# Attention scores of a tile in one two-bank buffer, and the softmax sum applied to the output

## The chip, the cores and the metric

The kernel runs on one core of a Trainium2 chip. The metric is the device time of one execution in microseconds (us). A core has TensorE (PE in the profile, its weight loads PEld), VectorE (DVE), ScalarE (ACT), GpSimd (POOL) and SyncE (SP, which issues most DMAs). Each engine runs its instructions in the order in which they stand and waits on semaphores for the others. TensorE writes to PSUM, which has eight banks of 512 float32 columns on each of 128 partitions.

## The reference

A trunk of two layers over 1024 positions of width 1024. Layer 0 mixes with two recurrent head groups (RWKV-7 and gated DeltaNet); layer 1 mixes with chunked attention. Each layer ends with an MLP and a gated per-layer embedding. The attention has 16 heads of 64. Queries and keys are normalised, and each chunk of 64 positions looks at itself and the eight chunks before it:

```python
rel = jnp.arange(CHUNK)[:, None] + pad - jnp.arange(band)[None, :]
bias = rel_bias[:, jnp.clip(rel, -C_MAX_REL, C_MAX_REL) + C_MAX_REL]
s = jnp.einsum('bqhd,bkhd->bhqk', q_c, k_b).astype(jnp.float32) + bias
s = jnp.where(valid, s, -jnp.inf)
prob = jax.nn.softmax(s, -1).astype(v.dtype)
return jnp.einsum('bhqk,bkhd->bqhd', prob, v_b)
```

The bias depends on the distance alone, and beyond 256 positions it is one constant for each head. Because softmax does not change when a constant is added to a whole row, that constant can be subtracted from all biases of a head.

## The kernel before

Only the attention stage of layer 1 matters here (`layer1_in`, L1590). Positions are taken in eight tiles of 128, two chunks each. A query tile m sees at most the five key tiles m-4 to m, with a masked quarter at each end. Heads are taken in pairs `pr`, and positions in halves `hf`, which gives 16 steps. A step has four blocks: two heads (`h`), and for each two query tiles (`blk`).

For a step, `attn_in` (L1680) computes q, k and v of a head pair for four tiles: 24 float32r matmuls of 384 columns into one of two dense banks (`dps`, `wq`), which ACT and DVE then read (`qk` L1713, `vs` L1717 and L1718). `attn_norm` (L1732) transposes q and k (also through a dense bank) and splits them into a high and a low part (`F`, `Ql`). `attn_block` (L1759) is the softmax block:

- For a query tile the scores of the last three key tiles, the near ones, go to a bank `sn` (two buffers); those of up to two far key tiles go to a bank `sf` (one buffer). Each score is two matmuls, against q's high and low part; `score` cuts a run of key tiles where the tile of normalised keys ends, every four key tiles.
- On the near scores DVE adds the bias table `toep` and takes the row maximum in one custom instruction, into the SBUF tile `pb` (L1809). The far scores have a constant bias, which POOL has subtracted from the table (L1767), so DVE only masks a corner (L1816) and takes their maximum (L1817). L1818 joins the two maxima and negates them (L1821 where there are no far scores).
- ACT takes the exponential of the far scores out of PSUM (L1819) and of the near ones in place (L1822), each with its row sum. DVE adds the sums (L1824) and takes the reciprocal of one column (L1825). ACT scales all of `pb` by it (L1826).
- TensorE transposes the probabilities into a bank `pt` (two buffers; L1846, recorded at L165). ACT rounds them to float32r and DVE subtracts (`ptile`, L317 and L318), and the output matmuls `po` accumulate values times probabilities (L1858, recorded at L161). After a head's second block ACT and DVE fold the two halves of `po` into `y` (L1867, L1868), and `y` is written out.

Two lanes take blocks in turn, so that one lane's softmax runs beside the other's and beside the dense matmuls of later steps. The program is written in the order that a small planner sets (`run`, L123): it counts the time of matmuls and, at each `yield`, lets a lane rest for the time in the table `LAT` (L34). `attn_block0` is the rest after each tile's softmax, `attn_block1` the rest before the transposes. A scheduler of the language then fixes each engine's order. Matmuls of all lanes are issued by the helpers at L161 and L165, so groups are told apart by their tiles. Behind the attention, from about 2385 us on, stand the dense stages of layer 1.

The eight PSUM banks of this stage are two dense ones, two `sn`, one `sf`, two `pt` and one `po` (tag `o`).

## Time and profile before

| | us |
|---|---|
| runs of the kernel: median (lowest to highest of 3) | 3195.7 (3192.25 to 3198.93) |
| profiled execution: span from the first to the last instruction | 3188.9 |
| what lies between that span and the runs' median | 6.8 |
| attention stage of layer 1 (1800 to 2385) | 585.0 |
| dense stages behind it (2385 to 3189) | 804.0 |

No time of its own is recorded for the profiled execution beside its span, so the median of the runs stands for it. In the profile's groups each row names the line, the engine, the operation, output tile <- input tiles, the shapes and the count, then the busy time and the mean of one instruction (ns), and then how long the engine sat idle just before them and on whom it waited. A row of the waits names who waited, for whom, the sum in us, how often and the longest.

### The profile page before, as it was taken

The numbers are of one execution on the slowest core, as the hardware profiler recorded it, in microseconds if no ns is written. First come the engines' busy times: TensorE is split into PE (matmuls) and PEld (weight loads), VectorE is DVE, ScalarE is ACT, GpSimd is POOL, SyncE is SP. The second block draws the span as 40 slices with busy tenths as digits, with TensorE's granted clock in tenths as the row PEclk, the third lists the DMA queues.
The fourth block names the chain that finished last, engine by engine and source line by source line (L and its number), as shares of the span: only waits on it lengthen the run. The fifth ranks groups of instructions, "written<-read, shape, count | busy, mean of one in ns | idle before, by whom it ended". The sixth has DMA issues, their size and how long they took to land.

```text
span 3188.9 us, 45834 instructions
## 1 busy us (share of the span) xinstructions
PE 3080.8 (97%) x17448; PEld 2580.6 (81%) x17448; DVE 2005.1 (63%) x4020; ACT 1405.7 (44%) x2640; POOL 531.1 (17%) x982
## 2 busy tenths in 40 slices
PE   7999999999999999999999899989999999999999
PEld 5887778877877888888888888888878888888887
DVE  6565675557748766655546576776768666655552
ACT  4343443334426555312123477777756554312121
POOL 6334443434500000000004210110200000000002
PEclk8999889999899999999999999999999999999999
DMA  3312112222336433523213210110256333522313
GB/s 121 94 60 63 47 40 71 64 62 78 119 107 200 148 122 109 189 94 105 93 53 126 70 36 32 48 39 16 76 177 215 139 119 109 190 100 93 106 47 106
DMA packets 144715, 309.58 MB, mean 97 GB/s; under 512 B 40944, under 2 KB 43120, under 8 KB 144496
## 3 DMA queue, kind: packets, MB, share of 16 engines
q1 hardware_dynamic: 126064, 273.10, 25.8%
q10 hardware_dynamic: 18432, 33.56, 2.7%
q8 instruction: 137, 2.24, 0.3%
q14 instruction: 82, 0.67, 0.1%
HBM read 232.16 MB, written 74.45 MB: 96 GB/s over the span
## 4 chain that ended last, share of the span: by engine, by line
PE 86%; DVE 8%; ACT 4%; DMA 1%; issue 1%; POOL 0%; SPq 0%; DVEq 0%; ACTq 0%
PE dps L161 71%; PE ch L161 2%; PE iz L161 2%; PE tp L161 1%; PE po L161 1%; PE pm L161 1%; PE py L161 1%; PE pt L165 1%; DVE ptile L318 1%; PE sn L161 1%; PE pp L161 1%; DVE pb L1809 1%; ACT pb L1822 1%; DMA wraw<-in_w_qkv 1%; PE sc L161 1%
## 5 line engine op out<-in xcount | busy, mean ns | idle before, releaser
L161 PE MATMUL dps<-r,act 128*128 128x512 f32 x3528 | 824.3, 392 | 0.0
L161 PEld LDWEIGHTS dps<-r,act 128*128 128x128 f32 x3528 | 662.1, 188 | 145.7
L161 PE MATMUL dps<-xg,whi 128*128 128x512 f32 x1280 | 435.1, 416 | 12.7 <-ACT xg L320 7.2
L161 PE MATMUL dps<-late,act 128*128 128x512 f32 x1536 | 352.9, 391 | 0.0
L161 PEld LDWEIGHTS dps<-late,act 128*128 128x128 f32 x1536 | 288.5, 188 | 63.1
L161 PE MATMUL dps<-wq,act 128*128 128x384 f32 x1536 | 304.5, 344 | 6.9 <-DVE vs L1718 3.5
L1466 POOL TENSOR_TENSOR pn<-pn,prs 128x512 f32<-128x512 f32 x32 | 45.2, 1415 | 1587.7 <-ACT prs L354 1492.5
L161 PEld LDWEIGHTS dps<-xg,whi 128*128 128x128 f32 x1280 | 245.1, 196 | 67.6 <-ACT xg L320 7.2
L161 PEld LDWEIGHTS dps<-wq,act 128*128 128x128 f32 x1536 | 265.5, 191 | 11.1 <-DVE vs L1718 5.5
L161 PE MATMUL dps<-xg,wlo 128*128 128x512 f32 x640 | 264.5, 414 | 1.5 <-DVE wlo L277 1.5
L1342 DVE TENSOR_TENSOR late<-late,dps 128x512 f32<-128x512 f32 x224 | 152.9, 685 | 150.9 <-PE dps L161 120.2
L1441 DVE TENSOR_TENSOR xw<-xw,dps 128x512 f32<-128x512 f32 x192 | 131.6, 686 | 148.5 <-PE dps L161 147.5
L1240 ACT CAST act<-act 128x1024 fp32r<-128x1024 f32 (+1 forms) x99 | 94.7, 963 | 284.9 <-DMA act<-in_w 158.2
L1240 ACT CAST act<-late 128x512 fp32r<-128x512 f32 x210 | 124.6, 618 | 140.5 <-PE dps L161 121.3
L1241 DVE TENSOR_TENSOR act<-late,act 128x512 fp32r<-128x512 f32 x210 | 139.9, 688 | 27.2 <-ACT act L1240 26.9
L161 PEld LDWEIGHTS dps<-xg,wlo 128*128 128x128 f32 x640 | 125.6, 196 | 28.0 <-DVE wlo L277 2.8
L161 PE MATMUL dps<-xw,act 128*128 128x512 f32 x576 | 138.9, 392 | 0.0
L276 ACT CAST whi<-wraw 128x1024 fp32r<-128x1024 f32 x78 | 81.6, 1046 | 120.6 <-PE dps L161 81.6
L161 PEld LDWEIGHTS dps<-xw,act 128*128 128x128 f32 x576 | 108.1, 188 | 24.1
L1241 DVE TENSOR_TENSOR act<-act 128x1024 fp32r<-128x1024 f32 (+1 forms) x99 | 109.9, 1115 | 20.8 <-ACT act L1240 20.1
L277 DVE TENSOR_TENSOR wlo<-wraw,whi 128x1024 fp32r<-128x1024 f32 x78 | 99.3, 1274 | 36.5 <-ACT whi L276 35.7
L161 PE MATMUL po<-ptile,vs 128*128 128x256 f32 (+1 forms) x576 | 103.7, 292 | 15.5 <-ACT ptile L317 7.1
(474 smaller groups left out, 5410.7 us busy)
## 6 DMA issues: line engine op xcount, KB each, us to landing
act<-in_w SPq DMA_DIRECT2D x68, 512.0 KB
hd<-late ACTq DMA_DIRECT2D x128, 256.0 KB
late<-in_w SPq DMA_DIRECT2D x60, 512.0 KB
wraw<-in_w_in SPq DMA_DIRECT2D x56, 512.0 KB
act<-hd SPq DMA_DIRECT2D x56, 512.0 KB
wraw<-in_w_out SPq DMA_DIRECT2D x21, 512.0 KB
wraw<-in_w_qkv SPq DMA_DIRECT2D x21, 512.0 KB
pn<-pnd SPq DMA_DIRECT2D x32, 256.0 KB
```

Source lines behind the costliest of these rows:

```text
L161: return self.nc.tensor.matmul(out, lhsT, rhs, start=start, stop=stop)
L165: return self.nc.tensor.transpose(out, in_, ident)
L276: nc.scalar.copy(hi, raw)
L277: nc.vector.tensor_tensor(lo, raw, hi.bitcast(F32), op=ALU.subtract)
L318: nc.vector.tensor_tensor(dst[:, 1, sl], src, dst[:, 0, sl].bitcast(F32), op=ALU.subtract)
L1240: A.copy(hi, s)
L1241: V.tensor_tensor(lo, s, hi.bitcast(F32), op=ALU.subtract)
L1342: V.tensor_tensor(r, t, u, op=ALU.add)
L1441: V.tensor_tensor(x[n][:, sl], x[n][:, sl], ps, op=ALU.add)
L1466: G.tensor_tensor(pn, pn, prs[:, sl], op=ALU.mult)
L1809: V.tensor_tensor_reduce(S, pn[:, 0:nn * P], toep[:, (3 - nn) * P:], op0=ALU.add, op1=ALU.max, scale=1.0, scalar=NEG, accum_out=mx[:, 0:1])
L1822: A.activation(S, S, AF.Exp, bias=mx[:, 2:3], accum_out=l[:, 0:1])
```

## The change

A query tile's scores, up to five key tiles or 640 columns, now go into one buffer `sc` of two adjoining PSUM banks. There is one such buffer. `score` cuts a run also where it would cross from the first bank to the second. The bias table covers all five key tiles (640 columns instead of 384), with both masked corners written into it, so that nothing is subtracted from it. One custom DVE instruction adds the bias and takes the maximum of the whole row, one DVE instruction negates it, and one ACT instruction takes the exponential of the whole row with its sum.

The probabilities are not scaled. Instead DVE writes the reciprocal of the sum, repeated over 64 columns, into a tile `rl` (a query tile's rows by the head's 64 columns). After both heads of a step, TensorE transposes the four 128x128 pieces of `rl` into a dense bank, and DVE multiplies the step's output `y` by it. The bank that is left goes to `pt`, which has three buffers. Two entries of the planner's table change.

```diff
-    "attn_block0": 0.97,
-    "attn_block1": 4.45,
+    "attn_block0": 1.70,
+    "attn_block1": 3.00,
...
-            rbl = l1.tile([P, 16], F32, tag="rbl", name="rbl", bufs=1)
-            nc.sync.dma_start(out=rbl, in_=a["rb_last"].rearrange("(o c) -> o c", o=1).broadcast_to((P, 16)))
...
-                t = l1.tile([P, 3 * P], F32, tag="toep", name="toep", bufs=3)
+                t = l1.tile([P, 5 * P], F32, tag="toep", name="toep", bufs=3)
...
             t = st["toep"][h]
-            G.tensor_scalar(t, t, rbl[:, 2 * pr + h:2 * pr + h + 1], None, op0=ALU.subtract)
-            G.memset(t[0:64, 320:384], NEG)
+            G.memset(t[0:64, 576:640], NEG)
+            G.memset(t[64:128, 0:64], NEG)
...
-                e = min(n - o, 4 - j % 4)
+                e = min(n - o, 4 - j % 4, 4 - o % 4)
...
+        if h == 0 and blk == 0:
+            st["rl"] = sm.tile([P, 4, P], F32, tag="rl", name="rl", bufs=2)
         for m in (m0, m0 + 1):
-            n0 = max(0, m - 2)
-            nn = m - n0 + 1
             f0 = max(0, m - 4)
-            nf = n0 - f0
-            pn = psm.tile([P, HB], F32, tag="sn", name="sn", bufs=2)
-            score(pn[:, 0:nn * P], m, n0, nn)
-            mx = sm.tile([P, 4], F32, tag="mx", name="mx", bufs=4)
+            n = m - f0 + 1
+            ps = psm.tile([P, 2 * HB], F32, tag="sc", name="sc")
+            score(ps, m, f0, n)
+            mx = sm.tile([P, 2], F32, tag="mx", name="mx", bufs=4)
             pb = self.wp.tile([P, 5 * P], F32, tag="pb", name="pb", bufs=4)
-            S = pb[:, nf * P:(nf + nn) * P]
-            V.tensor_tensor_reduce(S, pn[:, 0:nn * P], toep[:, (3 - nn) * P:], op0=ALU.add, op1=ALU.max,
+            S = pb[:, 0:n * P]
+            V.tensor_tensor_reduce(S, ps[:, 0:n * P], toep[:, (5 - n) * P:], op0=ALU.add, op1=ALU.max,
                                    scale=1.0, scalar=NEG, accum_out=mx[:, 0:1])
-            l = sm.tile([P, 4], F32, tag="l", name="l", bufs=4)
-            if nf:
-                pf = psm.tile([P, HB], F32, tag="sf", name="sf")
-                score(pf[:, 0:nf * P], m, f0, nf)
-                if m >= 4:
-                    V.memset(pf[64:128, 0:64], NEG)
-                V.reduce_max(mx[:, 1:2], pf[:, 0:nf * P], axis=AX.X)
-                V.tensor_scalar(mx[:, 2:3], mx[:, 0:1], mx[:, 1:2], -1.0, op0=ALU.max, op1=ALU.mult)
-                A.activation(pb[:, 0:nf * P], pf[:, 0:nf * P], AF.Exp, bias=mx[:, 2:3], accum_out=l[:, 1:2])
-            else:
-                V.tensor_scalar(mx[:, 2:3], mx[:, 0:1], -1.0, None, op0=ALU.mult)
-            A.activation(S, S, AF.Exp, bias=mx[:, 2:3], accum_out=l[:, 0:1])
-            if nf:
-                V.tensor_tensor(l[:, 0:1], l[:, 0:1], l[:, 1:2], op=ALU.add)
-            V.reciprocal(l[:, 2:3], l[:, 0:1])
-            A.activation(pb[:, 0:(nf + nn) * P], pb[:, 0:(nf + nn) * P], AF.Copy, scale=l[:, 2:3])
+            V.tensor_scalar(mx[:, 1:2], mx[:, 0:1], -1.0, None, op0=ALU.mult)
+            l = sm.tile([P, 1], F32, tag="l", name="l", bufs=4)
+            A.activation(S, S, AF.Exp, bias=mx[:, 1:2], accum_out=l)
+            V.reciprocal(st["rl"][:, m % 4, hs], l.broadcast_to((P, 64)))
...
-            pt = psm.tile([P, HB], F32, tag="pt", name="pt", bufs=2)
+            pt = psm.tile([P, HB], F32, tag="pt", name="pt", bufs=3)
...
             V.tensor_tensor(y[hs], po[hs], tmp[hs], op=ALU.add)
             if h == 1:
+                pn = self.bank()
+                for m in range(4):
+                    self.tr(pn[:, m * P:(m + 1) * P], st["rl"][:, m, :], self.ident)
+                V.tensor_tensor(y, y, pn, op=ALU.mult)
...
-    rel = np.arange(P)[:, None] + 2 * P - np.arange(3 * P)[None, :]
+    rel = np.arange(P)[:, None] + 4 * P - np.arange(5 * P)[None, :]
     out["rb"] = f["attn_rel_bias"][0][:, np.clip(rel, -256, 256) + 256]
-    out["rb_last"] = f["attn_rel_bias"][0][:, 512]
```

**Scores on TensorE.** The order on PE at the first head's first block of step 7 (`F1` keys, `F0` and `Ql` the parts of q; the number behind a name is its buffer's; in brackets the engines that it waits for). Before:

```order
L161 MATMUL sn_18508<-F1_18037,F0_18489 128x256 [waits Activation_49]
L161 MATMUL sf_18517<-F1_18037,F0_18489 128x256
L161 MATMUL sn_18541<-F1_18037,F0_18489 128x128
L165 MATMUL pt_18561<-ident_62,pb_18427 128x128 [waits Activation_49]
L165 MATMUL pt_18572<-ident_62,pb_18427 128x128 [waits DVE_49]
L161 MATMUL sn_18508<-F1_18037,Ql_15464 128x256 [waits DVE_49]
L161 MATMUL sn_18508<-F1_18476,F0_18489 128x128
L161 MATMUL sn_18508<-F1_18476,Ql_15464 128x128
L161 MATMUL sf_18517<-F1_18037,Ql_15464 128x256
L161 MATMUL sn_18541<-F1_18037,Ql_15464 128x128
L161 MATMUL sn_18541<-F1_18476,F0_18489 128x256
L161 MATMUL sn_18541<-F1_18476,Ql_15464 128x256
```

With the change, the same block:

```order
L161 MATMUL sc_18335<-F1_17896,F0_18306 128x512 [waits Activation_49]
L161 MATMUL po_18241<-ptile_18318,vs_17396 128x256 [waits Activation_49]
L161 MATMUL sc_18335<-F1_17896,Ql_15462 128x512 [waits DVE_49]
L161 MATMUL sc_18335<-F1_18293,F0_18306 128x128
L161 MATMUL sc_18335<-F1_18293,Ql_15462 128x128
L161 MATMUL po_18241<-ptile_18318,vs_17396 128x256 [waits DVE_49]
L161 MATMUL po_18241<-ptile_18318,vs_17396 128x256 x2
L161 MATMUL po_18241<-ptile_18328,vs_17396 128x256 [waits Activation_49]
L161 MATMUL po_18241<-ptile_18328,vs_17396 128x256 [waits DVE_49]
L161 MATMUL po_18241<-ptile_18328,vs_17396 128x128 x2
L161 MATMUL sc_18371<-F1_17896,F0_18306 128x384 [waits DVE_49]
L161 MATMUL sc_18371<-F1_17896,Ql_15462 128x384
```

The two near tiles and the far one stood interleaved, each in a bank of its own; now the second tile's scores wait for DVE behind the first's, and the output matmuls of another block stand between.

**From the transposes to the output matmuls.** PE at the first head's second block of step 12 (`pt` transposes of the probabilities `pb`, `ptile` their split). Before:

```order
L165 MATMUL pt_20817<-ident_62,pb_20695 128x128 [waits Activation_49]
L165 MATMUL pt_20817<-ident_62,pb_20670 128x128
L165 MATMUL pt_20817<-ident_62,pb_20695 128x128
L165 MATMUL pt_20832<-ident_62,pb_20695 128x128 x2
L161 MATMUL dps_20915<-wq1_20762,act_15376 128x384
L161 MATMUL dps_20915<-wq0_20761,act_15376 128x384
L161 MATMUL po_20683<-ptile_20822,vs_19964 128x256 [waits Activation_49]
L161 MATMUL po_20683<-ptile_20822,vs_19964 128x256 [waits DVE_49]
```

With the change, the transposes of the same block:

```order
L165 MATMUL pt_20465<-ident_62,pb_20356 128x128 [waits Activation_49]
L165 MATMUL pt_20465<-ident_62,pb_20330 128x128
L165 MATMUL pt_20465<-ident_62,pb_20356 128x128
L165 MATMUL pt_20476<-ident_62,pb_20356 128x128 x2
L161 MATMUL dps_20520<-wq0_20425,act_15146 128x384
L161 MATMUL dps_20520<-wq1_20426,act_15146 128x384
L161 MATMUL sc_20455<-F1_20173,F0_20192 128x256 [waits DVE_49]
L161 MATMUL sc_20455<-F1_20173,Ql_15461 128x256
L161 MATMUL dps_20520<-wq0_20425,act_15146 128x384
L161 MATMUL dps_20520<-wq0_20425,act_15220 128x384
L161 MATMUL dps_20520<-wq1_20426,act_15220 128x384
L165 MATMUL pt_20528<-ident_62,pb_20392 128x128 [waits PE_49,Activation_49]
```

Two dense matmuls stood between the last transpose and the first output matmul of that block. Now scores, dense matmuls and another block's transpose come first; the block's output matmuls stand further down.

**The reciprocals' transposes.** PE at the end of step 4, with the change, and DVE at the same place:

```order
L161 MATMUL po_17469<-ptile_17585,vs_16634 128x256 [waits Activation_49]
L161 MATMUL po_17469<-ptile_17585,vs_16634 128x256 [waits DVE_49]
L161 MATMUL po_17469<-ptile_17585,vs_16634 128x128 x2
L165 MATMUL dps_17622<-ident_62,rl_17195 128x128 [waits DVE_49]
L165 MATMUL dps_17622<-ident_62,rl_17195 128x128 x3
L161 MATMUL sc_17569<-F1_17120,F0_17544 128x512 [waits Activation_49]
L161 MATMUL sc_17569<-F1_17120,Ql_15462 128x512 [waits DVE_49]
L161 MATMUL sc_17569<-F1_17531,F0_17544 128x128
L161 MATMUL sc_17569<-F1_17531,Ql_15462 128x128
L161 MATMUL dps_17646<-wq0_17377,act_14852 128x384 [waits DVE_49]
```

```order
L318 TENSOR_TENSOR ptile_17562<-pt_17557,ptile_17562 128x512 [waits Activation_49]
L318 TENSOR_TENSOR ptile_17585<-pt_17581,ptile_17585 128x384 [waits Activation_49]
L1752 SCALAR_TENSOR_TENSOR F1_17531<-dps_17526,vecs_60,F1_17531 64x512 [waits Activation_49]
L1752 SCALAR_TENSOR_TENSOR Ql_15462<-dps_17539,d_qg8_85,F0_17544 64x512 [waits PE_49,Activation_49]
L1854 TENSOR_TENSOR y_17455<-po_17469,otmp_17619 64x512 [waits Activation_49]
L1859 TENSOR_TENSOR y_17455<-y_17455,dps_17622 128x512 [waits DVE_49,PE_49]
L1807 ISA pb_17575,mx_17574<-sc_17569,toep_16629 128x640 [waits PE_49]
```

The transposes of `rl` and the multiply are new. The dense matmuls of `dps_17646` wait for DVE: their bank is the one that the multiply (L1859) reads.

More of the change, by code (lines that the diff above doesn't have):

```diff
@@ L1608, in layer1_in @@
             jobs = iter([(s, h, b) for s in range(16) for h in range(2) for b in range(2)])
-            self.run([self.attn_lane(steps, jobs, l1, rbl) for _ in range(2)] + [self.attn_norms(steps, l1), self.attn_ins(steps, l1)])
+            self.run([self.attn_lane(steps, jobs, l1) for _ in range(2)] + [self.attn_norms(steps, l1), self.attn_ins(steps, l1)])
     def attn_ins(self, steps, l1):
@@ L1657, in attn_norms, with attn_lane @@
             self.mark(("in", s), self.lat["norm"])
-    def attn_lane(self, steps, jobs, l1, rbl):
+    def attn_lane(self, steps, jobs, l1):
         for s, h, b in jobs:
             yield ("in", s)
-            yield from self.attn_block(s, *steps[s], h, b, l1, rbl)
+            yield from self.attn_block(s, *steps[s], h, b, l1)
     def weights3(self, odd):
@@ L1757, in attn_norm, with attn_block @@
             yield "attn_norm0"
-    def attn_block(self, s, pr, hf, h, blk, l1, rbl):
+    def attn_block(self, s, pr, hf, h, blk, l1):
         nc, psm, sm = self.nc, self.psm, self.sm
```

## The prediction

> **What bounds the kernel now.** I read the page first, then the busy time by stages, then the waits of TensorE inside the one stage that the change touches, then its groups of instructions and the chain that ended last.
>
> ```profile
> span 3188.9 us, 45834 instructions
> PE 3080.8 (97%) x17448; PEld 2580.6 (81%) x17448; DVE 2005.1 (63%) x4020; ACT 1405.7 (44%) x2640; POOL 531.1 (17%) x982
> core 0: us, PE busy (x) PEld busy (x) DVE busy (x) ACT busy (x) POOL busy (x), PEclk, DMA share, GB/s
> 1800.00:2385.00 585.00, 538.77 (x3329) 496.72 (x3327) 417.27 (x1320) 426.55 (x991) 70.58 (x69) 0.98 0.18 59
> 2385.00:3189.00 804.00, 798.84 (x3500) 653.89 (x3499) 479.61 (x658) 287.78 (x434) 21.69 (x16) 1.00 0.35 123
> ```
>
> The attention stage runs from about 1800 to 2385 us. Even there PE is the busiest engine, but it is busy for 538.8 of 585 us; behind it, in the dense stage, for 798.8 of 804. So the stage holds some 46 us of PE idle, and DVE (417 us) and ACT (427 us) are both near three quarters full, on short chains that feed PE. What matters is which of these chains PE waits for. These are the waits of the weight loads (PEld) and then of the matmuls (PE) in that window: us in total, times, longest.
>
> ```profile
> PEld po L161 <- ACT ptile L317: 12.2, 18, 2.0
> PEld po L161 <- DVE ptile L318: 10.6, 18, 1.6
> PEld pt L165 <- ACT pb L1826: 9.3, 11, 1.9
> PEld sf L161 <- ACT pb L1819: 6.8, 15, 1.2
> PEld pt L165 <- DVE ptile L318: 3.7, 8, 0.5
> PEld sn L161 <- DVE mx L1809: 3.1, 15, 0.3
> PE po L161 <- ACT ptile L317: 7.1, 12, 1.8
> PE pt L165 <- ACT pb L1826: 6.7, 9, 1.8
> PE po L161 <- DVE ptile L318: 6.6, 13, 1.4
> PE pt L165 <- DVE ptile L318: 4.3, 8, 1.5
> PE sf L161 <- ACT pb L1819: 3.3, 7, 1.0
> ```
>
> Three of the five chains are touched: the transposes `pt` wait for the scaled probabilities (L1826) or for a free `pt` bank; the far scores `sf` wait until the exponential has read their only bank (L1819); the output matmuls `po` wait for the split of the transposes. A PE row begins only after the modelled end of the last matmul, a PEld row as soon as no weight is loading, so I price a removed wait by PEld and keep the PE rows as the lower bound.
>
> **The change part by part: TensorE's own work.** The spacing of matmuls is read from the chain of waits, where they run without a gap: start, us, what.
>
> ```profile
> 2001.32 0.46 PE pt L165 x4
> 2001.78 3.47 PE dps L161 x20
> 2005.26 0.40 PE sf L161 x4
> 2008.38 0.93 PE po L161 x8
> 2374.51 4.56 PE dps L161 x20
> ```
>
> That is 0.115 us for a transpose, 0.10 to 0.116 for 128 and 256 columns, 0.174 for 384 and 0.228 for 512. The order has the scores before as 192 matmuls of 128 columns, 192 of 256 and 128 of 384 (63.8 us), and now as 224, 96, 96 and 64 of 512 (64.8 us): +1.0. The new transposes of the reciprocals are 4 in each of 16 steps, 64 x 0.115 = +7.4. Together **+8.4 us** of PE work, in a stage where nothing hides PE.
>
> **DVE and ACT.** First groups by line with all shapes together, then single shapes: xcount, busy us, mean ns, idle before.
>
> ```profile
> L1826 ACT ACTIVATE pb<-pb,l 128x640 f32<-128x640 f32 (+4 forms) x128 | 86.4, 693 | 16.6 <-DVE l L1825 13.9 <-DVE ss L1727 1.6 <-DVE mx L1821 0.4
> L1819 ACT ACTIVATE pb<-sf,mx 128x256 f32<-128x256 f32 (+1 forms) x80 | 36.2, 452 | 42.0 <-DVE mx L1818 41.6
> L1819 ACT ACTIVATION_READ_ACCUMULATOR pb<-sf,mx 128x1 f32 x80 | 15.8, 197 | 0.0
> L1817 DVE TENSOR_REDUCE mx<-sf 128x1 f32<-128x256 f32 (+1 forms) x80 | 31.2, 390 | 0.9
> L1824 DVE TENSOR_TENSOR l<-l 128x1 f32<-128x1 f32 x80 | 13.2, 165 | 27.8 <-ACT pb L1822 27.5
> L1816 DVE MEMSET sf<- 64x64 f32 x64 | 7.2, 112 | 28.9 <-PE sf L161 28.4
> L1818 DVE TENSOR_SCALAR mx<-mx 128x1 f32<-128x1 f32 x80 | 16.6, 207 | 1.1
> L1821 DVE TENSOR_SCALAR mx<-mx 128x1 f32<-128x1 f32 x48 | 6.5, 144 | 0.3
> L1825 DVE RECIPROCAL l<-l 128x1 f32<-128x1 f32 x128 | 20.2, 160 | 8.2 <-ACT pb L1822 6.1
> L1867 ACT COPY otmp<-po 64x512 f32<-64x512 f32 x32 | 18.6, 581 | 3.5 <-PE po L161 2.7
> ```
>
> ```profile
> L1809 DVE CUSTOM_DVE_ANT_0 pb<-sn,toep 128x384 f32<-128x384 f32 x96 | 51.6, 551 | 8.9 <-PE pt L165 6.4 <-PE sn L161 1.8
> L1809 DVE CUSTOM_DVE_ANT_0 pb<-sn,toep 128x128 f32<-128x128 f32 x16 | 4.5, 281 | 2.5 <-PE pt L165 1.9 <-PE sn L161 0.6
> L1822 ACT ACTIVATE pb<-pb,mx 128x384 f32<-128x384 f32 x96 | 58.6, 610 | 4.3 <-DVE mx L1821 4.3
> L1826 ACT ACTIVATE pb<-pb,l 128x640 f32<-128x640 f32 x64 | 53.3, 833 | 15.6 <-DVE l L1825 13.5 <-DVE ss L1727 1.6
> L318 DVE TENSOR_TENSOR ptile<-pt,ptile 128x512 fp32r<-128x512 f32 x80 | 53.5, 683 | 11.0 <-ACT ptile L317 9.9
> ```
>
> ACT loses the scaling (86.4), the far exponential (36.2) and its sum (15.8). The one that is left grows from 384 to 640 columns; the 640-column row of L1826 stands for it, 833 - 610 = 0.22 us more, 64 times, and about half as much 16 times: +16. Net -122 us, 427 to about 304.
>
> DVE loses 31.2 + 13.2 + 7.2, and 80 x (207 - 144) ns = 5.0. The bias-and-maximum costs (551 - 281)/256 = 1.05 ns a column, so 640 columns take 0.82 us: +0.27 x 64 and +0.135 x 16 = 19.4. The multiply of the output is 16 times a 512-column row of 0.68: 11.0. The reciprocal now writes 64 columns, which the trace does not show. Below it costs what it costs now, 0.16. Above I put the 512-column row, 0.68, as if each column took eight. I take plain streaming, 0.16 + 64 x 1.05 ns = 0.23, because the one-column reciprocal is no dearer than the one-column add (160 against 165 ns): +8.6. Net about -18 us, at worst 128 x 0.52 = 67 us instead of 8.6, which is +41.
>
> The Trainium skill (VectorE: DVE Perf Modes, "First, the fixed hardware budget") speaks against the change here: it says that a reciprocal is an iterative divide with a repeat count of 8. By that, 64 columns would be 512 passes, an estimate of some 0.53 us at its 0.96 GHz; no run here shows a wide one yet.
>
> None of DVE's or ACT's busy time sets the end; it works through PE's waits. POOL loses 13 bias shifts off any chain, and the wider bias table is 128 KB more for each of 16 loads where DMA is 18% busy; I cost both at nothing.
>
> **Waits that go.** (1) `pt` on the probabilities. From a score's last matmul to a transposable tile was 0.55 + 0.39 + 0.21 + 0.45 + 0.20 + 0.61 + 0.20 + 0.17 + 0.16 + 0.83 = 3.8 us of instructions; now it is 0.82 + 0.14 + 0.83 + 0.20 = 2.0. The planner's gap shrinks too, from 0.97 + 4.45 = 5.4 to 1.70 + 3.00 = 4.7, so slack grows from 1.6 to 2.7: three quarters of 9.3, **-7.0**. (2) `pt` on a free bank: there are three, and in the new order no transpose of probabilities waits for DVE: **-3.7**. (3) The `sf` bank is gone: **-6.8**. (4) `po` on the split. Between the last transpose of a tile and the first output matmul that waits for ACT, the old order has under 1 us of PE work in 37 of 119 places, the new one in 13 of 125; for the DVE half it is under 2 us in 37 of 96 and now in 20 of 139. ACT's queue is also more than a quarter shorter. I take 60% of 12.2 + 10.6: **-13.7**. Sum -31.2; by the PE rows the same shares give -20.8.
>
> **Waits that come.** (5) There is one two-bank score buffer, so the next tile's first score matmul waits until DVE has read the last one, with all of PE's queue behind it. Before, `sn` had two buffers. Old order: 17 of 113 waits had under 1 us of PE work as cover, and 3.1 us were lost, which fits a turn of 0.92 us. The read is 0.27 longer now, a turn of 1.19; the new order has 16 of 121 under 1 us and 24 under 1.5, and the shortfalls to 1.19 sum to 9.7: **+6.6**. (6) The reciprocals' transposes hold one of the two dense banks until the output is multiplied. Copy 0.58, add and multiply 0.68 each, with the handovers 2.5 us; the next user of that bank comes 1.3 to 2.7 us of PE work after the last output matmul in five of the 16 steps, later elsewhere: shortfalls of **+3.5**.
>
> Sum: 8.4 - 31.2 + 6.6 + 3.5 = **-12.7 us**. On the span that is 3176.2. The median of the runs is 3195.7, 6.8 above this span, so I predict **3183 us**. With the PE rows for the removed waits it would be -2.3, 3193.
>
> **The rivals.** *More comes back.* All of (1) to (4) go, 42.6 instead of 31.2: -24, 3172. For it speaks that ACT loses more than a quarter of its work; against it, that DVE, which a third of these waits name, loses little.
>
> *DVE takes it back: no change.* If the reciprocal is near its upper bound, DVE goes to 458 of some 575 us, and a reciprocal stands in DVE's order ahead of the score read or the split that PE needs. A turn 0.5 longer in half of the score reads (their shortfalls at 1.7 us sum to about 22) adds 6, and about 4 on the split: -3, 3193. The skill's rule on the reciprocal would end here.
>
> *The single score buffer decides: slower.* With two lanes sharing it, one DVE instruction of 0.68 us ahead of the read makes the turn 2 us; 36 of 121 reads have less cover, and the shortfalls sum to 31.8, so +28.7 instead of +6.6. With the removed waits at their PE price: 8.4 - 20.8 + 28.7 + 3.5 = +20, 3215. It decides from a turn of about 1.5 us on. For it: DVE is 71% busy. Against it: the old `sn` waits show a longest of 0.3 us.
>
> **How the numbers follow.** A measurement of this kernel tells about 0.2%, 6.4 us, from no change. Forecast (-6.4 to -20, 3176 to 3189): 0.38. More: 0.19. No change: 0.23. Slower: 0.20. So faster 0.57, same 0.23, slower 0.20. The range takes in the larger gain with the waits for `vs` gone too (some 9 us below 3172) and most of the slower case: 3160 to 3212.
>
> **What would show it.** Right: no wait of `pt` on the score bank's readers or on DVE, `po` waits for ACT and DVE under 10 us together in the PEld rows, `sc` on the score read near 10 us, ACT near 300 us in the stage, and a stage some 13 us shorter with the work behind it unchanged. Wrong: `sc` waits of 20 us or more, a wide reciprocal near 0.6 us with waits behind it, or dense matmuls waiting for the output's multiply in most steps.

## The result and the profile after

The changed kernel takes 3177.97 us (median of 4 runs, 3171.28 to 3180.88) against 3195.55 of the kernel before beside it (4 runs, 3192.25 to 3198.93). The ratio is 0.9937, with a 95% interval of 0.9923 to 0.9951: 0.63% or some 20 us faster (by the medians 17.6). The forecast was 3183, a gain of 12.7.

The page of the changed kernel, the execution's span and the engines' busy time:

```profile
span 3176.5 us, 45473 instructions
PE 3082.7 (97%) x17480; PEld 2587.2 (81%) x17480; DVE 2028.7 (64%) x3812; ACT 1307.4 (41%) x2352; POOL 515.4 (16%) x982
```

The span is 12.4 us shorter, less than the runs say. The stage began 6.4 us later in this execution (1777.1 us against 1770.7), although the change touches nothing before it. The odd one is the execution of the kernel before: in the other 13 traces of this document the stage begins between 1771.3 and 1785.3 us. The changed kernel's profiled execution took 3178.18 us, 1.7 more than its span. If the kernel before has about as much between the two, its profiled execution took some 3191 us, less than any of its runs, and most of the 6.8 us between its span and its median is that. So I compare stages. The attention stage is taken from the first read of a query bank (`qk`) to the first load for the residual add behind it (L1250), a place in the program and not a time. Its windows, of the kernel before and then of the changed one, with the columns of the windows in the prediction:

```profile
1770.70:2388.50 617.80, 570.79 (x3510) 527.80 (x3509) 430.31 (x1349) 434.82 (x1011) 73.70 (x72) 0.98 0.18 58
```

```profile
1777.10:2373.00 595.90, 563.62 (x3519) 526.06 (x3518) 453.88 (x1138) 335.09 (x721) 58.48 (x72) 0.98 0.19 62
```

The stage is 21.9 us shorter and what follows it 3.1 longer (800.4 to 803.5): -18.8. The 3.1 are work that changed sides: 3496 matmuls stand behind the border instead of 3484, with 798.3 us of PE busy instead of 795.3. DVE works 23.6 us more and ACT 99.7 less. The weight loads' waits in this stage, after the change (engine, tile and line, what was waited for: us, times, longest):

```profile
PEld sc L161 <- DVE mx L1807: 7.7, 18, 1.0
PEld pt L165 <- ACT pb L1811: 7.0, 11, 1.8
PEld po L161 <- ACT ptile L317: 6.7, 11, 1.2
PEld po L161 <- DVE ptile L318: 4.2, 7, 1.2
...
PEld dps L161 <- DVE y L1859: 3.2, 5, 1.0
```

The output matmuls' waits for the split have halved (22.8 to 10.9). Those for the far bank and for a free `pt` bank are gone. The waits for the score buffer (`sc`) and for the output's multiply (`y`, L1859, which holds a dense bank) are new. The groups of the new work, shapes kept apart:

```profile
L1812 DVE RECIPROCAL rl<-l 128x64 f32<-128x64 f32 x128 | 69.7, 546 | 25.1 <-ACT pb L1811 24.6
...
L1811 ACT ACTIVATE pb<-pb,mx 128x640 f32<-128x640 f32 x64 | 53.4, 835 | 45.2 <-DVE mx L1809 44.8
L1807 DVE CUSTOM_DVE_ANT_0 pb<-sc,toep 128x640 f32<-128x640 f32 x64 | 52.0, 813 | 18.0 <-PE sc L161 17.4
```

The 640-column instructions cost what was predicted (0.83 and 0.82 us). The reciprocal of 64 columns does not: 546 ns, where I took 0.23.

**How the runs below are compared.** All runs stand in one table. "Against before" is the ratio to the kernel before in the same series, less one, times 3196 us; a ratio's interval is about 4.5 us to each side, so a difference between two rows of different series is known to some 6 us. The last four columns are of one profiled execution: the stage as above; the sum of all PEld waits in it; the clock loss, which is the stage's length times one less the granted clock, summed over slices of 20 us; and what is left.

| kernel | median us | ratio (95%) | against before | stage | PEld waits | clock loss | rest |
|---|---|---|---|---|---|---|---|
| before | 3195.6 | | | 617.8 | 73.5 | 12.4 | 531.9 |
| after | 3178.0 | 0.9937 (0.9923-0.9951) | -20 | 595.9 | 51.0 | 10.4 | 534.5 |
| e4_merge_only | 3152.9 | 0.9866 (0.9854-0.9879) | -43 | 567.5 | 36.0 | 1.8 | 529.7 |
| e3_defer_only | 3208.8 | 1.0044 (1.0029-1.0059) | +14 | 631.7 | 70.9 | 24.0 | 536.8 |
| e13_no_scale | 3147.8 | 0.9842 (0.9829-0.9856) | -50 | 561.8 | 32.0 | 1.8 | 528.0 |
| e10_wide_recip | 3168.6 | 0.9908 (0.9895-0.9922) | -29 | 586.8 | 51.3 | 8.8 | 526.7 |
| e6_one_recip | 3167.0 | 0.9913 (0.9899-0.9928) | -28 | 584.9 | 44.4 | 6.8 | 533.7 |
| e11_both | 3191.2 | 0.9981 (0.9970-0.9992) | -6 | 608.1 | 61.3 | 10.6 | 536.2 |
| e1_old_rests | 3167.4 | 0.9899 (0.9884-0.9914) | -32 | 585.1 | 42.0 | 8.8 | 534.3 |
| e12_merge_old_rests | 3158.4 | 0.9888 (0.9873-0.9903) | -36 | 578.4 | 45.1 | 6.8 | 526.5 |
| e2_before_new_rests | 3207.5 | 1.0034 (1.0022-1.0045) | +11 | 626.0 | 73.7 | 23.6 | 528.7 |
| e5_pt2 | 3182.3 | 0.9962 (0.9949-0.9976) | -12 | 597.8 | 57.7 | 3.6 | 536.5 |
| e8_pt1 | 3235.9 | 1.0132 (1.0117-1.0147) | +42 | 641.1 | 90.1 | 22.6 | 528.4 |
| e9_pt1_sc2 | 3275.4 | 1.0253 (1.0235-1.0271) | +81 | 683.5 | 109.8 | 61.8 | 511.9 |

The rest is the check on this split. In the six kernels that transpose the reciprocals it is 533.7 to 536.8 (mean 535.3), and in those that do not, e9 aside, 526.5 to 531.9 (mean 528.6). The difference of 6.7 is near the 7.4 us that the prediction gave the 64 transposes. In e9, 14.6 us of the clock loss fall inside waits and so are counted twice; counted once, its rest is 526.5, like the others, whose rests rise by 0 to 4 us in the same way. So stage times are PE's work, plus its waits, plus a clock that falls after waits.

### The profile page after: what moved, and what is told of

It is laid out like the page before. It is cut to its first block, busy times and chain, and to the rows that moved or that the text cites. A ratio compares the mean times of both kernels' runs of the same rounds, so it can differ in the third digit from the quotient of the medians.

```text
span 3176.5 us, 45473 instructions
## 1 busy us (share of the span) xinstructions
PE 3082.7 (97%) x17480; PEld 2587.2 (81%) x17480; DVE 2028.7 (64%) x3812; ACT 1307.4 (41%) x2352; POOL 515.4 (16%) x982
## 4 chain that ended last, share of the span: by engine, by line
PE 86%; DVE 7%; ACT 3%; DMA 2%; issue 1%; POOL 1%; SPq 0%; ACTq 0%; DVEq 0%; POOLq 0%
PE dps L161 71%; PE ch L161 2%; PE iz L161 2%; PE sc L161 2%; PE po L161 1%; PE tp L161 1%; PE pm L161 1%; PE py L161 1%; PE pt L165 1%; PE pp L161 1%; DVE pb L1807 1%; DVE ptile L318 1%; ACT pb L1811 0%; PE st L161 0%; PE dps L165 0%
## 5 line engine op out<-in xcount | busy, mean ns | idle before, releaser
L161 PEld LDWEIGHTS dps<-wq,act 128*128 128x128 f32 x1536 | 266.1, 191 | 11.4 <-DVE vs L1716 4.5
L1811 ACT ACTIVATE pb<-pb,mx 128x640 f32<-128x640 f32 (+4 forms) x128 | 89.5, 699 | 84.2 <-DVE mx L1809 82.1
L1241 DVE TENSOR_TENSOR act<-act 128x1024 fp32r<-128x1024 f32 (+1 forms) x99 | 109.8, 1114 | 22.5 <-ACT act L1240 21.8
```

Source lines behind the costliest of these rows:

```text
L161: return self.nc.tensor.matmul(out, lhsT, rhs, start=start, stop=stop)
L1241: V.tensor_tensor(lo, s, hi.bitcast(F32), op=ALU.subtract)
L1811: A.activation(S, S, AF.Exp, bias=mx[:, 1:2], accum_out=l)
```

## The experiments

### The change in its two halves

**The merge alone.** From the changed kernel: the scores stay in one buffer with one bias, maximum and exponential, but ACT scales the probabilities as before. The third `pt` bank and the new rests stay.

```diff
-            l = sm.tile([P, 1], F32, tag="l", name="l", bufs=4)
-            A.activation(S, S, AF.Exp, bias=mx[:, 1:2], accum_out=l)
-            V.reciprocal(st["rl"][:, m % 4, hs], l.broadcast_to((P, 64)))
+            l = sm.tile([P, 2], F32, tag="l", name="l", bufs=4)
+            A.activation(S, S, AF.Exp, bias=mx[:, 1:2], accum_out=l[:, 0:1])
+            V.reciprocal(l[:, 1:2], l[:, 0:1])
+            A.activation(S, S, AF.Copy, scale=l[:, 1:2])
...
-                pn = self.bank()
-                for m in range(4):
-                    self.tr(pn[:, m * P:(m + 1) * P], st["rl"][:, m, :], self.ident)
-                V.tensor_tensor(y, y, pn, op=ALU.mult)
```

> The changed kernel with the probabilities scaled on ACT again (one more 640-column ACT instruction a tile, a one-column reciprocal, no transposes of reciprocals, no multiply of the output): the merge of the scores and the third pt bank alone. Theory: the sf wait (6.8) and the pt wait on DVE (3.7) go, the score buffer costs 4.6, the matmuls 1, the chain is about 0.9 us shorter than before, half of (1) and (4), -8: about -13, 3183. Against the changed kernel PE has 7.4 less to do. Rival (ACT's relief carries the gain): with ACT back near 420 us the po waits for ACT stay at 12 and the whole is -5 or less, 3190 and above.

**The deferred scaling alone.** From the kernel before: ACT no longer scales, DVE writes the wide reciprocals, and the output is multiplied; the scores stay in two banks. The rest is the old code.

```diff
+        if h == 0 and blk == 0:
+            st["rl"] = sm.tile([P, 4, P], F32, tag="rl", name="rl", bufs=2)
...
-            V.reciprocal(l[:, 2:3], l[:, 0:1])
-            A.activation(pb[:, 0:(nf + nn) * P], pb[:, 0:(nf + nn) * P], AF.Copy, scale=l[:, 2:3])
+            V.reciprocal(st["rl"][:, m % 4, hs], l[:, 0:1].broadcast_to((P, 64)))
...
+                pn = self.bank()
+                for m in range(4):
+                    self.tr(pn[:, m * P:(m + 1) * P], st["rl"][:, m, :], self.ident)
+                V.tensor_tensor(y, y, pn, op=ALU.mult)
```

> The kernel before with one part of the change alone: the probabilities stay unscaled, the wide reciprocals are transposed and multiply the output; near and far scores keep their banks, pt its two. Theory (the gain is the sum of several removed waits, none of which stands for the whole): ACT loses the 86 us of scaling and the chain to the transposes 0.99 us, which is about half of the steps (1) and (4) of the prediction, -3 and -7; the 64 transposes cost 7.4 and the held dense bank 4 to 5. Sum near +1: 3191 to 3200. Rival (ACT's relief carries the gain): 3185 or less, with the po waits for ACT halved, 12.2 to about 6 us. In both the reciprocal takes 0.55 us as in the changed kernel.

The merge alone gains 43 us, and the deferral alone loses 14. Both lie outside what was expected of them (3183 and 3191 to 3200). On top of the merge the deferral loses 23 (from -43 to -20). So the merge, with the third `pt` bank and the rests that go with it, carries the whole gain, and the deferral, which the prediction had entered as relief, gives back half of it. The version without it, at 3152.9 us, beats both kernels. The stage windows and waits of the merge alone:

```profile
1779.70:2347.20 567.50, 546.69 (x3455) 513.16 (x3455) 400.61 (x1122) 412.66 (x849) 55.94 (x72) 1.00 0.19 65
```

```profile
PEld sc L161 <- DVE mx L1805: 5.8, 14, 0.8
...
PEld po L161 <- ACT ptile L317: 3.2, 9, 1.0
PEld po L161 <- DVE ptile L318: 2.8, 9, 0.5
PEld pt L165 <- ACT pb L1811: 2.7, 6, 1.2
```

and of the deferral alone:

```profile
1781.30:2413.00 631.70, 585.86 (x3561) 542.48 (x3560) 474.84 (x1362) 355.62 (x881) 73.03 (x72) 0.96 0.16 56
```

```profile
PEld po L161 <- ACT ptile L317: 11.7, 20, 1.7
PEld sf L161 <- ACT pb L1821: 10.1, 8, 2.4
PEld pt L165 <- DVE ptile L318: 8.9, 13, 1.1
PEld po L161 <- DVE ptile L318: 6.8, 13, 1.5
...
PEld pt L165 <- ACT pb L1821: 3.1, 5, 1.4
...
PEld pt L165 <- ACT pb L1824: 1.1, 2, 0.8
```

Read the two side by side. With the merge, ACT is still busy for 413 us, and `po` waits 3.2 us for it. With the deferral ACT falls to 356, 79 less than before, and `po` waits for it as long as ever, 11.7 against 12.2. So ACT's load is not what these waits hang on. DVE goes the other way: 401 with the merge, 475 with the deferral, where `pt` waits 8.9 us for DVE to free a bank (before: 3.7). In 7 of these 13 waits, with 4.2 of the 8.9 us, the wide reciprocal is the instruction that DVE ran directly before the split.

**The merge with nothing scaled.** From the merge alone: this kernel leaves the normalisation out altogether (neither scaled probabilities nor a multiplied output, and no reciprocal), to price the scaling on ACT and its short reciprocals.

```diff
-            V.reciprocal(l[:, 1:2], l[:, 0:1])
-            A.activation(S, S, AF.Copy, scale=l[:, 1:2])
```

> The merge alone without any division by the sum: neither the reciprocal nor the scaling of the probabilities is done, nor anything in their place, so the attention output is left unnormalised. It is the merge with a deferred scaling that costs nothing, and shows what the scaling on ACT (86 us busy) is worth. Theory A (hidden): 3150 to 3153, within 3 us of the merge alone. Theory B (the relief of ACT and a chain shorter by 1 us are worth about 10 us, as the prediction had it): 3143 or less, with the waits of PE for probabilities and splits (11.7 us by weight loads) halved.

Two of its waits:

```profile
PEld pt L165 <- ACT pb L1809: 6.9, 12, 0.9
...
PEld po L161 <- DVE ptile L318: 3.1, 8, 0.5
```

It is 8 us faster than the merge alone by the ratios (5 by the medians), which is hardly more than the uncertainty of 6. The work taken away is 87 us of ACT and 20 of DVE. The waits for probabilities and splits did not fall by half, as the theory of a relief had it: those of `pt` rose from 2.7 to 6.9. By this pair, relieving ACT behind the merge is worth about 8 us; a second pair, below, says 22.

### What the deferral costs

**128 wide reciprocals and nothing else.** From the merge alone: DVE also writes the wide reciprocals, whose result nobody reads.

```diff
+        if h == 0 and blk == 0:
+            st["rl"] = sm.tile([P, 4, P], F32, tag="rl", name="rl", bufs=2)
...
             A.activation(S, S, AF.Copy, scale=l[:, 1:2])
+            V.reciprocal(st["rl"][:, m % 4, hs], l[:, 0:1].broadcast_to((P, 64)))
```

> The merge alone with 128 wide reciprocals added behind the scaling: the 64-column reciprocal of the changed kernel is computed and read by nobody, so that DVE carries 128 x 0.55 us more off every chain. Theory A (DVE's load is what the deferred scaling costs): the changed kernel minus the version with one reciprocal a step was 7.7 us, so +8 over the merge alone, 3159 to 3163, with PE's waits for DVE (24 us by weight loads in the merge alone) near 32. Theory B (the wide reciprocal is idle filling, and the 7.7 came from where the transposes stand): 3153 to 3155.

**One reciprocal for a step.** From the changed kernel: the sums of a step go into eight columns, DVE takes one reciprocal of them, and POOL repeats it over the columns of `rl`.

```diff
-            st["rl"] = sm.tile([P, 4, P], F32, tag="rl", name="rl", bufs=2)
+            st["l8"] = sm.tile([P, 8], F32, tag="l8", name="l8", bufs=2)
...
-            l = sm.tile([P, 1], F32, tag="l", name="l", bufs=4)
-            A.activation(S, S, AF.Exp, bias=mx[:, 1:2], accum_out=l)
-            V.reciprocal(st["rl"][:, m % 4, hs], l.broadcast_to((P, 64)))
+            A.activation(S, S, AF.Exp, bias=mx[:, 1:2], accum_out=st["l8"][:, 2 * (m % 4) + h:2 * (m % 4) + h + 1])
...
+            if h == 1 and m % 4 == 3:
+                r8 = sm.tile([P, 8], F32, tag="r8", name="r8", bufs=2)
+                V.reciprocal(r8, st["l8"])
+                st["rl"] = sm.tile([P, 4, P], F32, tag="rl", name="rl", bufs=2)
+                G.tensor_copy(st["rl"].rearrange("p m (h c) -> p (m h) c", h=2),
+                              r8.rearrange("p (n o) -> p n o", o=1).broadcast_to((P, 8, 64)))
```

> The changed kernel with one reciprocal of eight columns a step in place of eight of 64 columns; GpSimd repeats the result over the columns, and the four transposes follow at the step's end. DVE loses 128 x 0.55 us and gains 16 short ones: -67 us. Theory (DVE is off the path, and only some of PE's waits name it): waits of PE for DVE (score read 7.7, split 4.2, output 5.2 by weight loads) fall by a third, 3 to 6 us under the changed kernel: 3172 to 3175. Rival A (the wide reciprocal had already taken back what the prediction missed): 10 us or more, 3168 or less. Rival B (a reciprocal off the chain costs nothing): 3178, or some us over it if the transposes in one piece at the end hold PE up.

**That, and the scaling kept on ACT too.** From the kernel with one reciprocal: ACT scales the probabilities by a one-column reciprocal again, and the output is multiplied by ones, so that all of the deferral's path on TensorE and DVE is there without its relief.

```diff
+            rc = sm.tile([P, 1], F32, tag="rc", name="rc", bufs=4)
+            V.reciprocal(rc, l)
+            A.activation(S, S, AF.Copy, scale=rc)
...
-                G.tensor_copy(...)
+                G.tensor_scalar(..., 0.0, 1.0, op0=ALU.mult, op1=ALU.add)
```

> The merge alone, scaled on ACT, and beside it the whole path of the deferred scaling with ones in it: the reciprocals of a step go to GpSimd, which writes ones in their place, TensorE transposes these (64 in all) and DVE multiplies the output by them. It differs from the version with one reciprocal a step by ACT's scaling alone, and from the merge alone by the transposes, the held dense bank and the multiply. Theory A (transposes, bank and multiply are the cost, ACT's scaling is hidden): as the version with one reciprocal, 3165 to 3169, and 13 us over the merge alone, of which 7.4 are the transposes. Theory B (ACT's scaling costs what the prediction's steps (1) and (4) took for it): 3178 to 3182.

The unread reciprocals, groups and waits in the kernel that has them beside the merge:

```profile
L1814 DVE RECIPROCAL rl<-l 128x64 f32<-128x64 f32 x128 | 68.1, 533 | 0.0
...
L1812 DVE RECIPROCAL l<-l 128x1 f32<-128x1 f32 x128 | 20.2, 158 | 17.3 <-ACT pb L1811 15.9
```

```profile
PEld sc L161 <- DVE mx L1807: 11.7, 16, 1.4
PEld po L161 <- DVE ptile L318: 6.8, 11, 1.2
```

The kernel with them takes 13 us more (-43 to -29), though nothing waits for them: DVE reads the scores later (`sc` 5.8 to 11.7) and splits later (`po` on DVE 2.8 to 6.8). That is more than either theory had. Taking them out of the changed kernel gives 8 us back (-20 to -28; 11 by the medians). Both have the same sign, and 8 to 13 us is the estimate of their price. The trace does not show how they act. The reciprocal is what DVE ran directly before the late instruction in only 3 of these 27 waits, with 1.6 of their 18.5 us; the rest may be DVE's fuller queue or the order that moved with the edit.

The larger part lies elsewhere. From the kernel with nothing scaled (-50) to the one with a single reciprocal (-28), what is added is the transposes, the multiply, and 16 reciprocals and POOL copies: 23 us. Of this 5.7 are TensorE's own work by the column of rests; waits rise by 12.4 and the clock loss by 5.0. The waits of the kernel with one reciprocal show where:

```profile
PEld po L161 <- DVE ptile L318: 11.3, 23, 0.9
```

With nothing scaled this row was 3.1. The multiply (L1863) does not hold these splits up itself: the trace has it among the four DVE instructions before the split in none of the 23 waits. In ten of them DVE itself was still waiting for ACT's half of the split; in the others it had just run other work, such as the split of q and k (L1752) or the fold of `y` (L1858). So the changed order of everything around it is what is left, and that is argued, not shown: no run holds the order fixed. The kernel with both scalings fits neither theory: it is 22 us above the one without ACT's scaling, and the same work taken from the merge alone was worth 8. In both pairs 128 short reciprocals on DVE go with the scaling. The largest wait here is on the score read, 3.6 us in the kernel without the scaling:

```profile
PEld sc L161 <- DVE mx L1807: 14.9, 19, 1.2
```

Why the scaling costs so much more here stays open, so what ACT's relief is worth is known only as 8 to 22 us.

### The planner's two numbers

The rests of `attn_block0` and `attn_block1` were set back to 0.97 and 4.45 in the changed kernel (e1) and in the merge alone (e12), and set to 1.70 and 3.00 in the kernel before (e2).

```diff
-    "attn_block0": 1.70,
-    "attn_block1": 3.00,
+    "attn_block0": 0.97,
+    "attn_block1": 4.45,
```

> The changed kernel with the planner's old rests (0.97 after a tile, 4.45 before the transposes). Theory A (buffers and chains carry the change, the rests place it): a tile's second scores come 0.7 us earlier behind the first's, into the single score buffer, so the score waits rise from 9 to about 15 us: 3180 to 3186. Theory B (the rests carry the gain): 3190 or more. Theory C (the rests do not matter): 3175 to 3180.

> The merge alone with the planner's old rests (0.97 and 4.45). In the changed kernel the old rests were worth 10 us. Theory A (these rests suit the merged scores better): 3142 to 3147, faster than the merge alone by 6 to 10. Theory B (the rests only shuffle the orders of the engines, and what comes of it differs in sign from kernel to kernel): anywhere in 3148 to 3165.

> The kernel before with the planner's new rests (1.70 and 3.00) and nothing else. Theory A (the rests as such gain nothing): within 10 us of the kernel before either way, 3187 to 3207; since its chain from scores to transposes is 3.8 us long, the shorter rest should raise the transposes' waits for probabilities (9.3 us by weight loads). Theory B (the rests carry the gain of the change): 3185 or less.

The new rests cost the changed kernel 12 us (-32 without them, -20 with them), gain the merge alone 7, and cost the kernel before 11. They don't carry the gain. In the changed kernel the old rests gave a time below all three theories: the score waits, which were to rise, stayed at 8.2 us, and those for probabilities fell from 7.0:

```profile
PEld pt L165 <- ACT pb L1811: 2.3, 5, 0.8
```

In the kernel before, the waits for probabilities rose with the shorter rest as expected, but only from 9.3 to 10.6. The three pairs also show how much a mere reordering is worth in this stage, about 7 to 12 us of either sign. In the kernel before they leave the sum of the waits alone (73.5 and 73.7) and the clock loss doubles (12.4 to 23.6). A difference of that size between two kernels whose edits also move the order cannot be given to the edit alone; this holds for the 8 to 13 us of the wide reciprocals too, which have only their two agreeing signs and the waits above for them. The 14 us that the deferral alone loses are hardly beyond it; the 43 and the 23 are.

### The banks

**Two `pt` banks** in the changed kernel, instead of three:

```diff
-            pt = psm.tile([P, HB], F32, tag="pt", name="pt", bufs=3)
+            pt = psm.tile([P, HB], F32, tag="pt", name="pt", bufs=2)
```

> The changed kernel with two pt banks instead of three (one bank lies idle). Theory: the pt wait on DVE comes back (3 to 4 us) and with it the short covers between transposes and output matmuls, half of the 12 us gained there: 8 to 10 us over the changed kernel, 3186 to 3188. Rival A (the third bank carries the whole gain): 3195. Rival B (it carries nothing): 3178, with no pt wait on DVE above 1 us.

It is 4 us slower by the medians and 8 by the ratios, between the theory and rival B and not clear of either. `pt` waits for a bank again, and the `po` waits stay:

```profile
PEld po L161 <- ACT ptile L317: 7.4, 10, 1.8
...
PEld po L161 <- DVE ptile L318: 4.0, 8, 1.1
...
PEld pt L165 <- DVE ptile L318: 1.9, 4, 0.8
```

The two `po` rows add to 11.4 against 10.9 in the changed kernel, so the third bank did not halve them. The merge alone was not run with two `pt` banks.

**One `pt` bank, and then two score buffers.** Two score buffers take four banks, which leaves `pt` one. Both kernels start from the merge alone, with `pt` at one bank: first with the one score buffer, then with two.

```diff
-            pt = psm.tile([P, HB], F32, tag="pt", name="pt", bufs=3)
+            pt = psm.tile([P, HB], F32, tag="pt", name="pt", bufs=1)
...
-            ps = psm.tile([P, 2 * HB], F32, tag="sc", name="sc")
+            ps = psm.tile([P, 2 * HB], F32, tag="sc", name="sc", bufs=2)
```

> The merge alone with one pt bank instead of three (two banks lie idle): the reference for the next run. Theory: every second transpose bank waits for its split, ACT's copy and DVE's subtract, 1.3 us, with waits of transposes for DVE of 30 us or more: 3180 to 3200. Rival (the order puts enough between): 3165 or less.

> The same with two score buffers (four banks) and one pt bank; it differs from the run with one pt bank by the second score buffer alone. Theory (the single score buffer costs what its waits show, 6 us by weight loads in the merge alone): 4 to 8 us under that run, with score waits on DVE under 2 us. Rival (the single buffer decides, as the slower rival of the prediction had it): 20 us or more under it.

One `pt` bank costs 85 us, and the second score buffer makes it 39 us slower, not faster; neither time was expected. The waits with one score buffer, and then with two:

```profile
PEld po L161 <- ACT ptile L317: 25.5, 46, 1.8
PEld pt L165 <- DVE ptile L318: 20.5, 43, 0.9
PEld sc L161 <- DVE mx L1805: 18.2, 34, 1.5
```

```profile
PEld po L161 <- ACT ptile L317: 44.0, 51, 3.7
PEld pt L165 <- DVE ptile L318: 22.2, 40, 1.3
PEld sc L161 <- DVE mx L1805: 15.5, 30, 1.4
```

The `sc` waits fall by only 2.7, and `po` loses 18 at the same time; the order changed with the buffers. The pair fails as a measurement of the single buffer: with one `pt` bank another wait decides. For the buffer's price there are only the rows of the changed kernel and of the merge.

## Why the prediction came out as it did

The direction was right, and the gain lies at the upper end of the forecast's own band of 6.4 to 20 us. The forecast was low: 12.7 of 18 to 20 us. Part of the closeness is luck: the predicted span of 3176.2 met 3176.5 only because the stage began 6.4 us later in this execution, and the sum came near because two halves that were not told apart, 43 us faster and 23 slower, were added. Term by term, in PEld waits of the stage:

| term | predicted | measured |
|---|---|---|
| TensorE's own work | +8.4 | +5.7 (rest +2.6, behind the stage +3.1) |
| (1) `pt` on the probabilities | -7.0 | -2.3 (9.3 to 7.0) |
| (2) `pt` on a free bank | -3.7 | -3.7 |
| (3) the far bank | -6.8 | -6.8 |
| (4) `po` on the split | -13.7 | -11.9 (22.8 to 10.9) |
| (5) one score buffer | +6.6 | +4.6 (3.1 to 7.7) |
| (6) a dense bank until the multiply | +3.5 | +3.2 (`dps` on `y` L1859) |
| all other waits | 0 | -5.6 |
| granted clock | 0 | -2.0 |
| sum | -12.7 | -18.8 |

The two terms of waits that could no longer occur, (2) and (3), were exact, and those worked out from the covers in the order, (4), (5) and (6), were off by 2 us or less. The gain beyond the forecast came from many small waits that I had not named, and a little from the clock and from TensorE's own work; (1) fell short by 4.7. All of it is one execution of each kernel.

**The step that failed was the reciprocal's price.** I took 0.23 us because one column costs no more than an add. One column shows only the fixed cost: from 1 to 64 columns the time goes from 160 to 546 ns, 6.1 ns for a column, against 1.05 in the bias-and-maximum. So the term of 8.6 us of DVE work should have been (546 - 160) x 128 = 49.4. With it, my sum for DVE gives +23 instead of -18, and 23.6 was measured. The Trainium skill names a repeat count of 8 for the reciprocal (VectorE: DVE Perf Modes, "First, the fixed hardware budget"). The estimate worked out from it, 0.53 us, is near the measured 0.546 as a total. By the column it is not: the same estimate gives 8.3 ns, where 6.1 was measured, and it has no fixed cost in it. The rival "DVE takes it back" had the size, 10 us where the runs say 8 to 13, and missed the end, because the merge's gain was large enough to bear it. Its mechanism, a reciprocal directly ahead of a score read or a split, stands behind only 7 of the 25 such waits in the changed kernel, with 3.0 of their 11.9 us.

**The reasons given for (4) do not hold.** I named ACT's shorter queue and, beside the order, counted on the split being less late for it. The deferral alone shortens ACT's queue by 79 us and the wait stays at 11.7; the merge alone leaves ACT busy for 413 us and the wait falls to 3.2. Nor is it the third `pt` bank. The covers in the order gave the size, so the order is what is left. Three pairs of kernels differ by the rests, and so by the order, alone: 10.9 us of these waits in the changed kernel and 7.6 with the old rests, 6.0 and 12.5 in the merge, 22.8 and 24.5 in the kernel before. So order by itself moves them by 2 to 7 us, less than the 11.9 that went. Every other edit moved the order too, and that it is the cause of the whole is argued, not shown.

**The mechanism of (1) holds for the old scores and not for the merged ones.** I priced this wait by the slack that the chain from a score to a tile that can be transposed leaves in the planner's gap. With near and far scores apart the wait follows it: 10.6 us at a slack of 0.9 (new rests), 9.3 at 1.6 (before) and 4.2 at 2.6 (the deferral alone, 3.1 and 1.1 in its two rows). With merged scores it does not. The merge alone has the longer chain, with a reciprocal of 0.16 and a scaling of 0.83 us more and so a slack of 1.7; it waits 2.7 us, but 6.4 beside the unread reciprocals. The changed kernel has 2.7 of slack and waits 7.0, and the kernel with nothing scaled 6.9. The old rests, with a slack of 3.4, bring 2.3. What sets this wait in the merged kernels stays open.

**What I left unsaid was that the change has two halves of opposite sign.** The merge alone brings all four terms of removed waits, without the deferral: (1) -6.6, (2) -3.7, (3) -6.8 and (4) -16.8 are -33.9 against the -31.2 foretold. Every gain that I gave the deferral, in (1) and (4), was to come from ACT, an engine busy for 70% of the stage. Every cost of it fell on TensorE and DVE, and with it the waits in (1) and (4) are 9.2 us longer again than in the merge alone.

ACT's fall was 100 us where I said 122, although the instructions cost what I said (138.4 removed, 16.7 added). Busy time counts overlapped instructions once: ACT's groups in the stage add to 496 us before and 370 after, its busy time is 435 and 335.

The single score buffer did not decide: its waits are 7.7 us, the longest 1.0, and not the 31.8 of that rival. That is so although DVE is 76% busy (453.88 of 595.90). Of the other signs named beforehand, transposes no longer wait for DVE; the `po` waits, 10.9, just missed the 10, and ACT, 335, missed the 300. Of the signs of being wrong, one came: the wide reciprocal near 0.6 us.

## What to carry to other kernels

A change with two halves is priced, and tried, by halves: here the merge (one bias, maximum and exponential for two of each, with the banks and rests that go with it) was worth twice what the whole change brought. Work taken from an engine that is not the bottleneck has no fixed price: the same 87 us from ACT, seven tenths busy, were worth 8 us in one pair of kernels and 22 in another. The price of a wide instruction of a slow kind cannot be read from a narrow one. Where a planner orders the work, try a few orders of the same code first: if they differ by 10 us, as here, so may two kernels for no other reason.

## What the hardware showed that I had not expected

**Waits can be paid a second time, through the clock.** The clock loss grows with the waits, but loosely: 32 and 36 us of waits go with 1.8 of loss, 42 to 61 with 4 to 11, 71 to 74 with 12 to 24, 90 with 23, 110 with 62. In these 14 traces the granted clock is either full or half, and at half for 3.41 us or a multiple of it within the stage. So a fall adds 1.7 us or more to the loss, and the loss counts the falls: one in the stage of the merge alone, five in that of the kernel before, eight there with the new rests and the same sum of waits. One such place in the kernel before, in windows of 2 us (columns as above, the granted clock third from the right):

```profile
1938.00:1940.00 2.00, 1.05 (x7) 0.76 (x7) 1.98 (x5) 1.28 (x4) 0.73 (x1) 1.00 0.53 213
1940.00:1942.00 2.00, 2.00 (x16) 1.91 (x15) 2.00 (x10) 0.82 (x4) 0.31 (x1) 1.00 0.00 0
1942.00:1944.00 2.00, 0.51 (x3) 0.30 (x2) 0.78 (x7) 2.00 (x8) 0.00 (x0) 1.00 0.00 0
1944.00:1946.00 2.00, 1.41 (x7) 0.93 (x7) 0.53 (x1) 1.93 (x5) 0.00 (x0) 0.75 0.00 0
1946.00:1948.00 2.00, 1.85 (x10) 1.79 (x9) 2.00 (x9) 0.37 (x1) 0.00 (x0) 0.50 0.00 0
1948.00:1950.00 2.00, 2.00 (x11) 2.00 (x11) 1.20 (x9) 1.93 (x7) 0.00 (x0) 0.50 0.00 0
1950.00:1952.00 2.00, 2.00 (x10) 1.90 (x10) 1.35 (x7) 2.00 (x7) 0.00 (x0) 0.55 0.00 0
1952.00:1954.00 2.00, 2.00 (x15) 1.97 (x15) 1.76 (x8) 1.95 (x7) 0.00 (x0) 1.00 0.03 8
```

TensorE is idle for 3.0 of the 8 us to 1946. The clock falls to half at 1945.0 and stays there for 6.8 us, although TensorE is nearly always busy again. That costs 3.4 us (0.5 + 1.0 + 1.0 + 0.9 over the windows), about as much as the idle time itself. The waits of TensorE from 1936 to 1952 us:

```profile
PE pt L165 <- ACT pb L1826: 1.8, 1, 1.8
PE po L161 <- ACT ptile L317: 1.1, 2, 0.8
```

The Trainium skill (TensorE: Matmul & The Clock Gate, "HAM oscillation — how this bites in real kernels") puts its rule as no idle gap of TensorE above some 3.4 us. Here the clock fell with no single wait above 1.8.

**One instruction reads across two PSUM banks at the usual rate.** The bias-and-maximum of 640 columns over two banks takes 813 ns, and of 384 columns in one bank 551: 1.02 ns for each column more, against 1.05 from 128 to 384 columns within one bank.
